# Output projection over head pairs, per-chunk scaling with a root taken as a power, and half-width masked products

## The chip, the cores and the metric

The kernel runs on one core of one Trainium2 chip. The metric is device time in microseconds (us) of one launch; the kernel before has a median of 3176.51 us in three runs. The engines go by the profile's names: PE is TensorE's matmul, PEld its weight load, DVE VectorE, ACT ScalarE, POOL GpSimd, SP the engine that issues most DMAs.

## What is computed

Two layers over 2048 tokens of width 1024, in float32. Layer 0 is a gated DeltaNet (GDN, 8 heads), layer 1 a gated linear attention (GLA, 4 heads); each head has key width 128 and value width 256. Cut to what the change touches:

```python
def gated_rmsnorm(o, w, gate):                 # per head, over its 256 values
    o = o * lax.rsqrt(jnp.mean(o * o, -1, keepdims=True) + RMS_EPS)
    return o * w * jax.nn.silu(gate)
def l2norm(t):                                 # q and k of GDN
    return t * lax.rsqrt(jnp.sum(t * t, -1, keepdims=True) + L2_EPS)
# mixer: p = x @ w_in (and a causal convolution of 4 taps for GDN); a recurrence over chunks gives o
y = gated_rmsnorm(o, norm_w, gate).reshape(B, T, heads * 256) @ w_out
x = layer_norm(DEEP_ALPHA * x + y, ln_g[i], ln_b[i])
```

## The kernel before

Work is cut into 48 units. A unit is one head of one layer on a group of 512 tokens, that is four chunks of 128 tokens (`NC`). There are 32 GDN units (4 groups, 8 heads) and 16 GLA units (4 groups, 4 heads). `PHASES` (L949) interleaves the layers: groups 0 and 1 of GDN, group 0 of GLA, and so on.

Four generators give the instructions (L936): `gemms` (input projection, convolution, gates), `preps` (what a head's recurrence needs: decays, inverses, masked products), `chains` (the recurrence itself) and `outs` (output projection, layer norm). `Plan.run` (L50 to L110) keeps a clock that adds up estimated matmul costs; a generator yields the time at which its next matmul can run, the first of the four that is due goes on, and `gemms` fills the rest. So the order in which each engine gets its instructions is fixed before the kernel runs, by the plan's costs (`COST`, L130) and by `O_GAP`, the least distance of two output groups. Every operation is issued inside the helper `Planned.call`, so the profile gives line L121 for all of them, and they are told apart by tile names.

Most products are float32 split in a high and a low part of a faster format (float32r): `mm3` (L234) issues three matmuls, high by high, high by low, low by high. Small products inside a head are plain float32, which the trace shows as two passes per matmul.

Tiles and names that the prediction's steps use:

- `wc`: a chunk of the input weights, both parts, 128 rows by up to 256 or 272 columns, in a ring of `W_BUFS` = 16. `Stream.load` (L261) brings the next chunk when one is free. The first time a weight is used it comes raw (`wraw`, ring of `RAW_BUFS` = 4), ACT makes the high part and POOL the low part, and the result is kept in DRAM (`wk`); later uses load that. `xh`, `xl` are the two parts of the transposed input, made by ACT and DVE from `woraw`.
- `psg` (three banks), `psc` (three), `psh` (one), `pso` (one): PSUM tiles of the projection, of a head's small products, of the recurrence and of the output projection.
- `gdn_prep` (L574): sums of squares of k and q go to `ss` (ACT), their inverse roots to `rr` (DVE, `rsqrt`); a 128 by 128 lower-triangular inverse is doubled from blocks of 16 to 128 with masked products `psc<-U,D` and `psc<-W,Tm` (L643 to L653 for the step from 16 to 32, at full width). `gla_prep` (L677) builds the intra-chunk matrix `At` over seven levels (L741 to L749); the levels with halves of 2, 4, 8 and 16 multiply full 128 by 128 tiles and merge what a mask picks with DVE's copy_predicated.
- `gdn_chain` (L790) and `gla_chain` (L815): per chunk, a read of the state (`psh<-S,kq`), `Rt` (DVE), `psh<-Rt`, `wt` (ACT copy), two products, and the new state `S` (DVE). `output` (L785) then takes the chunk's sum of squares (ACT Square into `junk`, `ssq`) and `og` = o times gate (DVE).
- `chains` (L828): after the fourth chunk, `z` = the RMS factor of all four chunks in one `rsqrt` on DVE (L834 to L845); `og` is transposed by PE and split to `oth`, `otl`. This waits in the plan until the unit before has finished its output projection.
- `outs` (L861): for each unit and each half `e` of the 1024 outputs, for each of four token tiles: two `mm3` (6 matmuls) into `pso`, then DVE computes y = pso * z + y. The weights `wo` (1024 KB with both parts, ring of `WO_BUFS` = 2) are loaded one ahead. After the last head of a group comes `layer_norm` (L918): bn_stats, bn_aggr, `rsqrt` of the variance on DVE, ACT scale and shift, DVE multiply and POOL add.
- `rsqrt` (L215): 11 DVE operations, two on the bits and three Newton steps of three, on tiles of 1, 4 or 8 columns:

```python
        v.tensor_scalar(yi, a.bitcast(I32), 1, None, ALU.logical_shift_right)
        v.tensor_scalar(yi, yi, -1.0, float(0x5F3759DF), ALU.mult, ALU.add)
        for _ in range(3):
            v.tensor_tensor(tmp, y, y, ALU.mult)
            v.scalar_tensor_tensor(tmp, tmp, -0.5, a, ALU.mult, ALU.mult)
            v.scalar_tensor_tensor(y, tmp, 1.5, y, ALU.add, ALU.mult)
```

Of the kernel before, what the change touches and what calls it, by code (L numbers as in the profile page):

```python
# [16 lines left out]
P = 128  # L17
# [7 lines left out]
DV = 256  # L25
QKV = 4096
ALPHA = 4.0 ** 0.25
BIG = 1.0e30
LEVELS = (1, 2, 4, 8, 16, 32, 64)
# [104 lines left out]
def trunk(ctx, tc, x, xT, w_in1, conv, a_log, dt_bias, nw1, w_out1, w_in2, gk_up, gk_b, nw2, w_out2,  # L134
# [46 lines left out]
    gkb = T("gkb", [P, H2])  # L181
    up = T("up", [80, 512], dt=F32R)
# [11 lines left out]
    def setup():  # L194
        sync.dma_start(nalog[:], a_log.unsqueeze(0).broadcast_to([P, H1]))
        sync.dma_start(dtb[:], dt_bias.unsqueeze(0).broadcast_to([P, H1]))
        sync.dma_start(cst[:].rearrange("p a b -> p (a b)"), consts)
        sync.dma_start(nws[0][:], nw1)
        s.activation(nalog[:], nalog[:], AF.Exp)
        v.tensor_scalar(nalog[:], nalog[:], -1.0, None, ALU.mult)  # L200
        v.tensor_reduce(id16[:], ident.rearrange("p (a b) -> p b a", b=16), mybir.AxisListType.X, ALU.add)
        for t in S1 + S2 + [halo]:
            v.memset(t[:], 0.0)

    def setup_gla():
        sync.dma_start(nws[1][:], nw2)
        sync.dma_start(gkb[:], gk_b)
        raw = T("th", [P, 512], 2)
        v.memset(raw[:], 0.0)
        for r0 in (0, 32, 64):  # L210
            sync.dma_start(raw[r0:r0 + 16, :], gk_up)
        s.copy(up[:], raw[:80, :])
        v.tensor_tensor(up[64:80, :], raw[64:80, :], up[64:80, :].bitcast(F32), ALU.subtract)

    def rsqrt(y, a, tmp):  # L215
        yi = y.bitcast(I32)
        v.tensor_scalar(yi, a.bitcast(I32), 1, None, ALU.logical_shift_right)
        v.tensor_scalar(yi, yi, -1.0, float(0x5F3759DF), ALU.mult, ALU.add)
        for _ in range(3):
            v.tensor_tensor(tmp, y, y, ALU.mult)  # L220
            v.scalar_tensor_tensor(tmp, tmp, -0.5, a, ALU.mult, ALU.mult)
            v.scalar_tensor_tensor(y, tmp, 1.5, y, ALU.add, ALU.mult)
# [26 lines left out]

    def prefetched(specs, load, ahead=1):  # L250
        ready = []
        specs = iter(specs)

        def take(ahead=ahead):
            while len(ready) <= ahead:
                spec = next(specs, None)
                ready.append(None if spec is None else load(spec))
            return ready.pop(0)
        return take
# [170 lines left out]
    take_wo = prefetched([c for u in units[:-1] for c in u.wo_specs()], load_wo)  # L430
# [142 lines left out]

    def gdn_prep(u):  # L574
# [16 lines left out]
        ss, r, tmp = small("ss", 2 * NC), small("rr", 2 * NC), small("rtmp", 2 * NC)  # L591
# [10 lines left out]
        v.tensor_scalar(ss[:], ss[:], 1e-6, None, ALU.add)  # L602
        rsqrt(r[:], ss[:], tmp[:])
        rk = r[:, 0:NC]
        rqs, brk, br2, s1 = (small(k, NC) for k in ("rqs", "brk", "br2", "s1"))
        v.tensor_scalar(rqs[:], r[:, NC:], float(P) ** -0.5, None, ALU.mult)
# [41 lines left out]
        d = PS("c", [P, NC, P])  # L648
# [26 lines left out]
        u.prep = dict(qd=qd, kd=kd, Bt=D2, Uf=Uf, s1=s1, rqs=rqs)  # L675

    def gla_prep(u):  # L677
# [63 lines left out]
        for lv, half in list(enumerate(LEVELS))[1:]:  # L741
            nxt = scaled(lv + 1) if lv + 1 < len(LEVELS) else None
            d = PS("c", [P, NC, P] if half < 32 else [P, NC, half])
            yield ready(d, E)
            if half < 32:
                for n in range(NC):
                    c = slice(n * P, (n + 1) * P)
                    mm(d[:, n], E[:, c], E[:, c])
                v.copy_predicated(At[:], bc(C(C_LV + lv), 1, NC).bitcast(I32), d)  # L749
            else:  # L750
                starts = range(0, P, 2 * half)
                for r0 in starts:
                    lo, hi = slice(r0, r0 + half), slice(r0 + half, r0 + 2 * half)
                    for n in range(NC):
                        e = E[:, n * P:(n + 1) * P]
                        mm(d[lo, n], e[:, lo], e[:, hi])
                for r0 in starts:
                    lo, hi = slice(r0, r0 + half), slice(r0 + half, r0 + 2 * half)
                    s.copy(At[lo, :, hi], d[lo])
            E = nxt  # L760
# [67 lines left out]
    def chains():  # L828
        for u in units:
            yield from after(("prep", u.at), ("vg", u.at))  # L830
            og, ssq = T("og", [P, NC, DV], 1), small("ssq", NC)
            yield from (gdn_chain if u.kind == 0 else gla_chain)(u, og, ssq)
            mark("rec", u.at)
            ms, z, tmp = small("ms", NC), small("z", NC), small("ztmp", NC)  # L834
            if u.kind == 1:
                v.tensor_scalar(ms[:], ssq[:], 1.0 / DV, 1e-6, ALU.mult, ALU.add)
                rsqrt(z[:], ms[:], tmp[:])
                v.tensor_scalar(z[:], z[:], 0.5 / ALPHA, None, ALU.mult)
            else:
                rqs = u.prep["rqs"][:]  # L840
                v.tensor_tensor(ms[:], rqs, rqs, ALU.mult)
                v.scalar_tensor_tensor(ms[:], ms[:], 1.0 / DV, ssq[:], ALU.mult, ALU.mult)
                v.tensor_scalar(ms[:], ms[:], 1e-6, None, ALU.add)
                rsqrt(z[:], ms[:], tmp[:])
                v.scalar_tensor_tensor(z[:], z[:], 0.5 / ALPHA, rqs, ALU.mult, ALU.mult)  # L845
            u.z = z
            end = u.at + 1 == len(units)
            if u.at and not end:
                yield from after(("out", u.at - 1))
            u.oT = []  # L850
            for j in range(2):
                d = PS("c", [P, NC, P])
                yield ready(d, og)
                transposes(d, lambda n: og[:, n, j * P:(j + 1) * P], NC)
                hi = T("D1" if end else "oth", [P, NC, P], 2, F32R)
                lo = T("D2" if end else "otl", [P, NC, P], 2, F32R)
                split(hi[:], lo[:], d)
                u.oT.append((hi, lo))
            mark("oT", u.at)

    def outs():  # L861
        for u in units:
            if u.first:
# [3 lines left out]
            end = u.at + 1 == len(units)  # L867
            wo = {}
            if u.at + 2 == len(units):
                wo = {e: take_wo(0) for e in range(2)}  # L870
                last = units[-1]
                yield from after(("vg", last.at))
                last_wo = {e: last_wo_parts(spec) for e, spec in enumerate(last.wo_specs())}
                gb = load_gb(last)
            if end:
                wo = last_wo
            yield from after(("oT", u.at))
            spaced = 0.0
            for e, n in [(e, n) for n in range(NC) for e in range(2)] if end else [(e, n) for e in range(2) for n in range(NC)]:
                final = u.last and e  # L880
                if e not in wo:
                    if final:
                        gb = load_gb(u)
                    wo[e] = take_wo(0 if final else WO_AHEAD)
                c = slice(e * 512, (e + 1) * 512)
                d = PS("g" if u.at + 2 >= len(units) else "o", [P, 512])
                for j in range(2):
                    hi, lo, _ = wo[e][j]
                    yield max(ready(d, u.oT[j][1], wo[e][j][2]), 0.0 if u.at + 2 >= len(units) or j else spaced)
                    if j == 0:  # L890
                        spaced = plan.clock + O_GAP
                    mm3(d, u.oT[j][0][:, n, :], u.oT[j][1][:, n, :], hi, lo, j == 0, j == 1)
# [4 lines left out]
            mark("out", u.at)  # L897
# [20 lines left out]
    def layer_norm(u, n, y, gb):  # L918
        st, mv = T("lnst", [P, 2, 6], 2), T("lnmv", [P, 2], 2)
        va, rs, tmp, mr = (small(k, 1, LN_BUFS) for k in ("lnva", "lnrs", "lntmp", "lnmr"))  # L920
# [3 lines left out]
        v.tensor_scalar(va[:], mv[:, 1:2], 1e-5 / ALPHA ** 2, None, ALU.add)  # L924
        rsqrt(rs[:], va[:], tmp[:])
# [14 lines left out]
W_BUFS, RAW_BUFS = 16, 4  # L940
WO_BUFS, WO_AHEAD, WO_RAW_BUFS = 2, 1, 4
# [48 lines left out]
```

## Time and profile before

| | us |
|---|---|
| three timed runs: lowest, median, highest | 3173.44, 3176.51, 3183.77 |
| the profiled execution, its own time | 3171.91 |
| span of its instructions | 3170.0 |
| PE busy (share of the span) | 3042.3 (96%) |
| PEld busy | 2578.7 (81%) |
| DVE busy | 2223.1 (70%) |
| ACT busy | 1181.8 (37%) |
| POOL busy | 388.8 (12%) |
| mean granted TensorE clock | 0.989 |

Busy time is the time in which at least one instruction of the engine was under way; matmuls overlap each other, so a busy PE may still be slower than it could be. Rows of a group read: line, engine, operation, output tile, input tiles, shape, count, busy time, mean ns of one, and the idle time of the engine just ahead of them with what ended it. Rows of the timeline read: start, duration, engine, operation, count, and in brackets the idle time before it and what ended that. Rows of waits give the total, the count and the longest.

### The profile page before, as it was taken

What the parts mean: (1) busy time and instruction counts of PE and PEld (TensorE: products, weight loads), DVE (VectorE), ACT (ScalarE), POOL (GpSimd) and SP (SyncE); (2) the same over time, 40 slices, a digit from 0 to 9 for tenths busy, and PEclk for the clock granted to TensorE, in tenths of its full rate; (3) what the DMA queues carried; (4) which work ended last, traced back from release to release, by engine and by line L of the source; (5) the groups of instructions that cost most, each with busy time, mean ns of one, the idle gap of its engine ahead of it and who ended that gap; (6) DMA issues with size and microseconds to landing.
All of it is one profiled execution on the core that took longest, in us unless ns stands there. A gap on an engine that the chain in (4) does not pass through costs nothing. (4 is left out here: it accounts for less than half of the span.)

```text
span 3170.0 us, 52680 instructions
## 1 busy us (share of the span) xinstructions
PE 3042.3 (96%) x18430; PEld 2578.7 (81%) x18430; DVE 2223.1 (70%) x6201; ACT 1181.8 (37%) x3091; POOL 388.8 (12%) x642
## 2 busy tenths in 40 slices
PE   9899999989999998998999999999999999999997
PEld 6678878778888877887888888888788888898895
DVE  6787777777677667578677757657877675755577
ACT  4444443332333445433333324523333233433331
POOL 4423220010000323102000000100200000100011
PEclk9999999999999999999999999999999999999998
DMA  7876565574444747665544553755645454465442
GB/s 236 258 238 213 183 194 180 162 223 150 141 131 146 226 125 250 215 201 184 163 143 141 152 167 101 232 179 164 192 148 155 153 159 131 152 193 173 147 161 105
DMA packets 442489, 551.93 MB, mean 174 GB/s; under 512 B 37568, under 2 KB 381888, under 8 KB 430192
## 3 DMA queue, kind: packets, MB, share of 16 engines
q1 hardware_dynamic: 412656, 505.57, 51.4%
q10 hardware_dynamic: 29568, 43.00, 4.0%
q8 instruction: 145, 2.38, 0.3%
q14 instruction: 120, 0.98, 0.1%
HBM read 421.24 MB, written 127.21 MB: 173 GB/s over the span
## 5 line engine op out<-in xcount | busy, mean ns | idle before, releaser
L121 PE MATMUL psg<-xh,wc 128*128 128x512 f32 x2560 | 886.9, 407 | 4.1 <-ACT wc L121 2.9
L121 PE MATMUL psg<-wc,xh 128*128 128x256 f32 (+1 forms) x4096 | 780.3, 289 | 24.3 <-DVE sg L121 14.3
L121 PEld LDWEIGHTS psg<-wc,xh 128*128 128x128 f32 x4096 | 654.4, 190 | 51.6 <-DVE sg L121 15.9
L121 PE MATMUL psg<-wc,xl 128*128 128x256 f32 (+1 forms) x2048 | 581.6, 284 | 0.0
L121 PEld LDWEIGHTS psg<-xh,wc 128*128 128x128 f32 x2560 | 480.2, 189 | 110.2 <-POOL wc L121 4.6
L121 PE MATMUL pso<-wo,oth 128*128 128x512 f32 x1472 | 506.8, 422 | 19.5 <-DVE y L121 17.0
L121 PE MATMUL psg<-xl,wc 128*128 128x512 f32 x1280 | 517.0, 404 | 0.4 <-DVE xl L121 0.3
L121 DVE SCALAR_TENSOR_TENSOR y<-pso,z,y 128x512 f32<-128x512 f32 x368 | 274.9, 747 | 188.8 <-PE pso L121 172.2
L121 PEld LDWEIGHTS psg<-wc,xl 128*128 128x128 f32 x2048 | 389.7, 190 | 1.3
L121 DVE SCALAR_TENSOR_TENSOR acc<-pb,taps,acc 128x512 f32<-128x512 f32 x384 | 301.6, 786 | 61.3 <-ACT acc L121 55.4
L121 PEld LDWEIGHTS pso<-wo,oth 128*128 128x128 f32 x1472 | 253.0, 189 | 67.7 <-DVE y L121 25.3
L121 PE MATMUL pso<-wo,otl 128*128 128x512 f32 x736 | 296.1, 402 | 0.5 <-DVE otl L121 0.5
L121 PEld LDWEIGHTS psg<-xl,wc 128*128 128x128 f32 x1280 | 241.8, 189 | 51.6 <-DVE xl L121 1.3
L121 POOL TENSOR_TENSOR wc<-wraw,wc 128x256 fp32r<-128x256 f32 (+1 forms) x288 | 231.4, 819 | 419.1 <-ACT wc L121 392.7
L121 ACT ACTIVATE th<-psg 128x256 f32<-128x256 f32 (+1 forms) x256 | 107.9, 434 | 349.5 <-PE psg L121 311.7
L121 ACT ACTIVATE junk<-psc 128x128 bf16<-128x128 f32 (+1 forms) x448 | 143.6, 321 | 219.6 <-PE psc L121 172.9
L121 DVE SCALAR_TENSOR_TENSOR sg<-th,psg 128x256 f32<-128x256 f32 x192 | 79.4, 415 | 145.6 <-ACT th L121 126.2
L121 POOL TENSOR_TENSOR y<-y,woraw 128x512 f32<-128x512 f32 x62 | 91.5, 1488 | 711.9 <-DVE y L121 324.4
L121 PEld LDWEIGHTS pso<-wo,otl 128*128 128x128 f32 x736 | 138.7, 188 | 37.1 <-DVE otl L121 6.1
L121 ACT ACTIVATE D<-D 128x512 f32<-128x512 f32 x160 | 100.0, 631 | 178.0 <-DVE D L121 140.2
L121 ACT COPY pb<-psg 128x512 f32<-128x512 f32 x128 | 74.9, 585 | 234.7 <-PE psg L121 227.7
L121 ACT CAST wc<-wraw 128x256 fp32r<-128x256 f32 (+1 forms) x288 | 112.1, 404 | 132.0 <-DMA wraw<-in_w_in 64.3
(182 smaller groups left out, 4454.5 us busy)
## 6 DMA issues: line engine op xcount, KB each, us to landing
wc<-wk SPq DMA_DIRECT2D x816, 256.0 KB
wk<-wc SPq DMA_DIRECT2D x272, 256.0 KB
wraw<-in_w_in SPq DMA_DIRECT2D x288, 128.0 KB
wo<-k_in_w_out SPq DMA_DIRECT2D x27, 1024.0 KB
wo<-_in_w_out SPq DMA_DIRECT2D x22, 1024.0 KB
wo<-ok_in_w_out SPq DMA_DIRECT2D x21, 1024.0 KB
Arep<-blk SPq DMA_DIRECT2D x32, 512.0 KB
wc<-wk SPq DMA_DIRECT2D x48, 272.0 KB
```

The source lines that it names most:

```text
L121: ins = op(*args, **kw)
```

## The change

1. **Pairs of units in the output projection.** `outs` goes over jobs: 23 pairs of units and two single units at the end. For each token tile and half `e`, four `mm3` (12 matmuls) of two heads accumulate in one bank, and one DVE add takes it to y. The scaling by `z` is gone from there. `WO_BUFS` is 3 and three `wo` tiles are asked for ahead; a job needs four, and the fourth is loaded only when its first half (`e` = 0) is done. `oth` and `otl` get four buffers each (`OT_BUFS`), and `chains` waits for the job of the unit two before.
2. **The root as a power, per chunk.** `rsqrt` is now an add of eps and a tensor_tensor with ALU.pow and a tile of -0.5 on POOL: 32 `rr`, 32 `lnrs` and 192 `z`. `z` is taken for each chunk right after its Square, from `ssq` and (for GDN) `qn`, a small DVE product of q's sum of squares, and ACT multiplies `og` by it. The constant factor moves to the `nw` tiles.
3. **Half width.** The step from 16 to 32 in `gdn_prep` and the levels 2 to 16 in `gla_prep` keep only those columns of the moving operand that the mask lets through: 64 in place of 128. The stationary operand stays 128 by 128. The DVE operations on these results have half the columns.
4. **Rings.** `W_BUFS` goes from 16 to 10, `RAW_BUFS` from 4 to 3. At the start, SP issues the fourth `wraw` load behind six more loads of `xT` and of small tables where it was the seventh DMA, and `cst` (the constants) is issued ahead of the seventh `wraw`.

The counts: PE 15923 instructions in the program before and after, DVE 6203 and 4566, ACT 2765 and 2957, POOL 647 and 1159, SP 1822 and 1822.

```diff
-    def rsqrt(y, a, tmp):
-        yi = y.bitcast(I32)
...
+    def rsqrt(y, a, eps):
+        if eps:
+            g.tensor_scalar(y, a, eps, None, ALU.add)
+        g.tensor_tensor(y, y if eps else a, mhalf[:, :y.shape[1]], ALU.pow)
...
+    jobs = [units[i:i + 2] for i in range(0, len(units) - 2, 2)] + [units[-2:-1], units[-1:]]
...
+    def later_half(a, sz):
+
+        if len(a.shape) == 2:
+            return a.rearrange("p (m h j) -> p m h j", h=2, j=sz)[:, :, 1, :]
+        return a.rearrange("p n (m h j) -> p n m h j", h=2, j=sz)[:, :, :, 1, :]
+
+    def halves(a, sz):
+        return a.rearrange("p n (m j) -> p n m j", j=sz)
...
-        v.tensor_scalar(ss[:], ss[:], 1e-6, None, ALU.add)
-        rsqrt(r[:], ss[:], tmp[:])
...
+        rsqrt(r[:], ss[:, :NC], 1e-6)
...
+        v.tensor_scalar(qn[:], ss[:, NC:], 1e-6, P * DV * 1e-6, ALU.add, ALU.mult)
...
         for n in range(NC):
-            mm(d[:, n], A[:, n], U[:, n])
-        v.tensor_tensor(W2[:], d, bc(C(C_LV + 4), 1, NC), ALU.mult)
-        d = PS("c", [P, NC, P])
+            mm(d[:, n], A[:, n], Uh[:, n])
+        v.tensor_tensor(Wh, d, bc(later_half(C(C_LV + 4), 16), 1, NC), ALU.mult)
+        d = halves(PS("c", [P, NC, P // 2]), 16)
         yield ready(d, W2)
         for n in range(NC):
-            mm(d[:, n], Tm[:, n], W2[:, n])
-        v.tensor_tensor(U[:], U[:], d, ALU.subtract)
+            mm(d[:, n], Tm[:, n], Wh[:, n])
+        v.tensor_tensor(Uh, Uh, d, ALU.subtract)
...
                 for n in range(NC):
-                    c = slice(n * P, (n + 1) * P)
-                    mm(d[:, n], E[:, c], E[:, c])
-                v.copy_predicated(At[:], bc(C(C_LV + lv), 1, NC).bitcast(I32), d)
+                    mm(d[:, n], E3[:, n], later_half(E3, half)[:, n])
+                v.copy_predicated(later_half(At[:], half), bc(later_half(C(C_LV + lv), half), 1, NC).bitcast(I32), d)
...
-        s.activation(jk[:], do, AF.Square, accum_out=ssq[:, n:n + 1])
+        c = slice(n, n + 1)
+        s.activation(jk[:], do, AF.Square, accum_out=ssq[:, c])
         v.tensor_tensor(og[:, n, :], do, u.sg[:, n, :], ALU.mult)
+        z = small("z", 1, 4)
+        if u.kind == 1:
+            g.tensor_scalar(z[:], ssq[:, c], DV * 1e-6, None, ALU.add)
+        else:
+            g.tensor_tensor(z[:], ssq[:, c], u.prep["qn"][:, c], ALU.add)
+        g.tensor_tensor(z[:], z[:], mhalf[:, :1], ALU.pow)
+        s.activation(og[:, n, :], og[:, n, :], AF.Copy, scale=z[:])
...
-            if u.at and not end:
-                yield from after(("out", u.at - 1))
+            if u.at >= 2 and not end:
+                yield from after(("out", units[u.at - 2].job))
...
+            parts = [(w, j) for w in job for j in range(2)]
             for e, n in [(e, n) for n in range(NC) for e in range(2)] if end else [(e, n) for e in range(2) for n in range(NC)]:
...
+                for k, (w, j) in enumerate(parts):
+                    hi, lo, wo = wos[w.at, e][j]
+                    yield max(ready(d, w.oT[j][1], wo), 0.0 if late or k else spaced)
...
+                    mm3(d, w.oT[j][0][:, n, :], w.oT[j][1][:, n, :], hi, lo, k == 0, k == len(parts) - 1)
                 y = ys[n]
-                v.scalar_tensor_tensor(y[:, c], d, u.z[:, n:n + 1], y[:, c], ALU.mult, ALU.add)
+                v.tensor_tensor(y[:, c], d, y[:, c], ALU.add)
+                if n == NC - 1 and not end:
+                    freed += len(job)
+                    if not final:
+                        fill()
...
-        v.tensor_scalar(va[:], mv[:, 1:2], 1e-5 / ALPHA ** 2, None, ALU.add)
-        rsqrt(rs[:], va[:], tmp[:])
+        rsqrt(rs[:], mv[:, 1:2], 1e-5 / ALPHA ** 2)
...
-W_BUFS, RAW_BUFS = 16, 4
-WO_BUFS, WO_AHEAD, WO_RAW_BUFS = 2, 1, 4
+W_BUFS, RAW_BUFS = 10, 3
+WO_BUFS, WO_RAW_BUFS, OT_BUFS = 3, 4, 4
```

How this moves the instructions is shown at two places. The first is ACT in the recurrence of a GDN unit, where `junk` is the Square, `wt` the copy that the next product waits for and `blk` a DMA that ACT issues. Before, it reads:

```order
L121 ACTIVATE junk_12049,ssq_11956<-psc_12044 128x256
L121 COPY wt_12064<-psh_12052 128x256
L121 ACTIVATE junk_12071,ssq_11956<-psc_12066 128x256
L121 COPY wt_12079<-psh_12074 128x256
L121 ACTIVATE junk_12110,ssq_11956<-psc_12081 128x256
L121 DMA blk_2717_12100<-X_12097 128x64
L121 COPY wt_12118<-psh_12113 128x256
L121 ACTIVATE junk_12125,ssq_11956<-psc_12120 128x256
```

And after, in the recurrence of a unit of the same kind:

```order
L122 ACTIVATE junk_9576,ssq_9496<-psc_9565 128x256
L122 ACTIVATE og_9495<-og_9495,z_9579 128x256
L122 COPY wt_9588<-psh_9583 128x256
L122 ACTIVATE junk_9613,ssq_9496<-psc_9590 128x256
L122 DMA blk_2198_9603<-X_9600 128x64
L122 ACTIVATE og_9495<-og_9495,z_9616 128x256
L122 COPY wt_9625<-psh_9620 128x256
L122 ACTIVATE junk_9632,ssq_9496<-psc_9627 128x256
L122 ACTIVATE og_9495<-og_9495,z_9635 128x256
L122 COPY wt_9644<-psh_9639 128x256
```

Between a Square and the next `wt` there is now the scaling of `og`, which waits for POOL's `z` of the same Square. In the whole program a scaling stands directly behind its Square 92 times of 192, and a `wt` directly behind a scaling 63 times of 128.

The second place is PE at one group of the output projection, where `oth` and `otl` are the two parts of the transposed `og`. Before, a group is two `mm3`:

```order
L121 MATMUL pso_6819<-wo_6445,oth_6432 128x512 x2
L121 MATMUL pso_6819<-wo_6445,otl_6433 128x512
L121 MATMUL pso_6819<-wo_6445,oth_6441 128x512
L121 MATMUL psc_6830<-W_1531_6365,Tm_6363 128x128 x4
L121 MATMUL pso_6819<-wo_6445,oth_6441 128x512
L121 MATMUL pso_6819<-wo_6445,otl_6442 128x512
```

And after, it is four, with two `wo` tiles (the last `mm3` of the group, on `oth_6951`, stands three rows after the last one shown here):

```order
L122 MATMUL pso_6982<-wo_5744,oth_6342 128x512 x2
L122 MATMUL pso_6982<-wo_5744,otl_6343 128x512
L122 MATMUL psg_6911<-xl_6204,wc_6633 128x512
L122 MATMUL psg_6911<-xh_6203,wc_6633 128x512
L122 MATMUL pso_6982<-wo_5744,oth_6351 128x512 x2
L122 MATMUL pso_6982<-wo_5744,otl_6352 128x512
L122 MATMUL psg_6911<-xh_6215,wc_6656 128x512
L122 MATMUL psg_6911<-xl_6216,wc_6656 128x512
L122 MATMUL psg_6911<-xh_6215,wc_6656 128x512
L122 MATMUL pso_6982<-wo_6135,oth_6942 128x512 x2
L122 MATMUL pso_6982<-wo_6135,otl_6943 128x512
```

The number of output matmuls is the same; the bank `pso` changes hands after 12 of them where it was 6.

More of the change, by code (lines that the diff above doesn't have):

```diff
@@ L866, in outs @@
                             else (lambda n: x2[u.gi][n][:]))
[L867 to L870, printed above, removed]
+            end, late = u.at + 1 == len(units), u.at + 2 >= len(units)
+            if late and not end:
                 last = units[-1]
                 yield from after(("vg", last.at))
[L873 removed]
+                for e, spec in enumerate(last.wo_specs()):
+                    wos[last.at, e] = last_wo_parts(spec)
@@ L919, in layer_norm @@
         st, mv = T("lnst", [P, 2, 6], 2), T("lnmv", [P, 2], 2)
-        va, rs, tmp, mr = (small(k, 1, LN_BUFS) for k in ("lnva", "lnrs", "lntmp", "lnmr"))
+        rs, mr = (small(k, 1, LN_BUFS) for k in ("lnrs", "lnmr"))
         for e in range(2):
```

92 lines of the change are left out of this document (39 added, 53 removed).

## The prediction

> **What bounds the kernel now.** I read the page first, for which engine is full.
>
> ```profile
> span 3170.0 us, 52680 instructions
> PE 3042.3 (96%) x18430; PEld 2578.7 (81%) x18430; DVE 2223.1 (70%) x6201; ACT 1181.8 (37%) x3091; POOL 388.8 (12%) x642
> ```
>
> PE is busy 96% of the span, so a change pays only where PE idles (3170.0 - 3042.3 = 128 us) or where PE's own work gets shorter. The second view, busy times by stretches (columns: length, PE, PEld, DVE, ACT, POOL, clock, DMA share, GB/s), tells where PE idles.
>
> ```profile
> 0.00:200.00 200.00, 175.17 (x946) 139.53 (x947) 137.35 (x316) 94.76 (x265) 85.95 (x129) 0.97 0.84 260
> 800.00:1000.00 200.00, 199.78 (x1167) 165.70 (x1166) 141.84 (x420) 65.19 (x200) 5.46 (x27) 1.00 0.48 144
> 3000.00:3170.00 170.00, 146.06 (x910) 128.03 (x909) 120.83 (x334) 45.63 (x97) 20.03 (x14) 0.94 0.42 140
> ```
>
> The first and the last stretch hold 24.8 + 23.9 = 49 us of it, a stretch in the middle 0.2 us, though DVE is busy 142 of 200 us there. The third view, what PE and its weight loads waited for (total, times, longest), names the releasers.
>
> ```profile
> PE pso L121 <- DVE y L121: 17.0, 18, 2.2
> PE psg L121 <- DVE sg L121: 15.8, 7, 7.2
> PE psc L121 <- DVE U L121: 14.5, 7, 5.7
> PE psh L121 <- DVE S L121: 14.0, 11, 3.2
> PE psg L121 <- ACT wc L121: 5.9, 5, 1.9
> PE psg L121 <- POOL wc L121: 3.4, 8, 1.0
> ```
> ```profile
> PEld psh L121 <- DVE S L121: 27.8, 47, 3.6
> PEld pso L121 <- DVE y L121: 25.3, 28, 2.5
> PEld psc L121 <- DVE U L121: 22.9, 29, 6.2
> ```
>
> DVE lies behind 61 us of PE's idle time in four rows, arriving weight chunks behind 9. A weight load stands earlier than the matmul behind it, while the last matmul's modelled end still counts as busy; what a wait really costs lies between the two rows, and I use their middle: y 21, S 21, U 19.
>
> **DVE's load.** These groups of DVE are touched.
>
> ```profile
> L121 DVE SCALAR_TENSOR_TENSOR y<-pso,z,y 128x512 f32<-128x512 f32 x368 | 274.9, 747 | 188.8 <-PE pso L121 172.2 <-issue 11.6
> ...
> L121 DVE SCALAR_TENSOR_TENSOR z<-ztmp,z 128x4 f32<-128x4 f32 x144 | 23.7, 164 | 2.9
> ...
> L121 DVE TENSOR_TENSOR W<-psc,cst 128x512 f32<-128x512 f32 x32 | 22.0, 689 | 13.2 <-PE psc L121 11.8
> ...
> L121 DVE TENSOR_SCALAR ms<-ssq 128x4 f32<-128x4 f32 x16 | 2.6, 163 | 0.0
> ```
> ```profile
> L121 DVE TENSOR_TENSOR og<-psc,sg 128x256 f32<-128x256 f32 x192 | 80.7, 421 | 9.2 <-ACT junk L121 6.5
> L121 DVE COPY_PREDICATED D<-cst,psc 128x512 f32<-128x512 int32 x64 | 47.0, 735 | 57.9 <-PE psc L121 57.9
> ```
>
> Evictions: 368 become 184, each of the kind of the 689 ns row, 127 us; 274.9 - 127 = -148. The root: 24 groups of small operations go, from `z<-ztmp,z` (23.7) to `ms<-ssq` (2.6), together 260 us; 32 `qn` at about 0.16 come back, 5. Half width: 64 operations of 689 ns go to the 421 ns of 256 columns, -17; 64 of 735 ns lose at most half, -23. Sum -148 - 255 - 17 - 23 = -443: DVE at about 1780 us, 56% of the span. None of this is the forecast, since it lies beside PE's work. What it buys is in the waits.
>
> **Waits on y (half of the hand-overs go).** Half as many at the same odds is -10 of 21; a DVE a fifth less loaded shortens the rest, -4. I take -14; bounds 0 (pairs wait as often) and -21.
>
> **Waits on sg, S and U (shorter queues on DVE).** `sg`, the gate's product, frees `psg`. Its longest wait is where a layer norm runs.
>
> ```profile
> 1494.90 1.23 DVE L121 SCALAR_TENSOR_TENSOR lnmr<-lnmv,lnrs 128x1 f32<-128x1 f32 x1
> ```
> ```profile
> 1493.13 2.98 POOL L121 TENSOR_TENSOR y<-y,woraw 128x512 f32<-128x512 f32 x2
> ```
> ```profile
> 1496.16 1.52 ACT L121 ACTIVATE y<-y,lnmr,lnrs 128x512 f32<-128x512 f32 x2 [3.09 <-DVE lnmr L121]
> ```
> ```profile
> 1502.97 0.80 PE L121 MATMUL psg<-wc,xh 128*128 128x256 f32 x2 [7.21 <-DVE sg L121]
> ```
>
> The root runs between other DVE work, `lnmr` comes late, ACT stands 3.09 us, and the gate behind it frees PE's bank 7.21 us late. With the root on POOL these steps leave DVE; but the next tile's pow stands behind the two POOL adds of the tile before, 2.98 us, so only part is won: -6 of 15.8. S and U are 40 us together, with DVE a fifth less loaded -9; bounds 0 and -20, half.
>
> **Half-width products: nothing on PE.** They are 512 matmuls, 1024 passes. Three bursts of the timeline tell what a pass costs.
>
> ```profile
> 46.93 0.53 PE L121 MATMUL psc<-lgz,cst 128*128 128x32 f32 x4
> ```
> ```profile
> 1043.94 1.05 PE L121 MATMUL psc<-U,D 128*128 128x128 f32 x8
> ```
> ```profile
> 1053.84 0.68 PE L121 MATMUL psc<-U,D 128*64 128x64 f32 x8
> ```
>
> With a stationary operand of 128 x 128, 32 moving columns took 0.53/4 = 0.133 us a pass and 128 columns 1.05/8 = 0.131; with 64 stationary columns it is 0.085. So a pass goes with the stationary operand, which stays at 128. I take 0; bounds 0 and 1024 x 0.046 = -47. The Trainium skill, "TensorE: Matmul & The Clock Gate", section "Back-to-back issue gap", gives an isolated gap of N / 2.4 + 2.5 ns, by which 64 columns fewer would save an estimated 27 ns a pass, 27 us in all; the same page's "LDWEIGHTS" section lets the load grow with the stationary columns, and this trace sides with that.
>
> **The root on POOL, and ACT held behind it (the added wait).** One turn of a GDN recurrence:
>
> ```profile
> 1002.17 0.38 ACT L121 ACTIVATE junk<-psc 128x256 bf16<-128x256 f32 x1 [1.28 <-PE psc L121]
> ...
> 1002.46 0.20 ACT L121 ACTIVATION_READ_ACCUMULATOR junk<-psc 128x1 f32 x1
> ...
> 1005.43 0.37 ACT L121 COPY wt<-psh 128x256 f32<-128x256 f32 x1 [2.78 <-DVE X L121]
> ...
> 1006.60 0.48 DVE L121 SCALAR_TENSOR_TENSOR S<-S,eg,psh 128x256 f32<-128x256 f32 x1 [0.52 <-PE psh L121]
> ...
> 1006.63 0.24 POOL L121 COPY X<-id 128x64 f32<-128x64 f32 x1 [38.41 <-DMA blk<-X]
> ```
> ```profile
> L121 ACT ACTIVATE y<-y,lnmr,lnrs 128x512 f32<-128x512 f32 x64 | 48.3, 806 | 79.0 <-DVE lnmr L121 49.3 <-DVE lnrs L121 21.6 <-POOL y L121 6.3
> ...
> L121 ACT ACTIVATE D<-U,brk 128x128 f32<-128x128 f32 x128 | 40.9, 390 | 1.0
> ```
> ```profile
> L121 POOL TENSOR_TENSOR y<-y,woraw 128x512 f32<-128x512 f32 x62 | 91.5, 1488 | 711.9 <-DVE y L121 324.4 <-DMA wc<-wk 246.5 <-DVE lnva L121 101.6
> ```
>
> The sum of squares is there at 1002.66, the next `wt` starts at 1005.43: 2.77 us. Into it must fit POOL's add, POOL's pow and ACT's scaling of 128x256 (between 390 and 806 ns, 0.5). That leaves 2.2 us for two POOL operations and some hand-overs. The trace has no pow; its nearest rows are a small copy at 0.24 us and a two-input add of 512 columns at 1.49. One column is nearest to the copy: 0.25 for the add, 0.4 for the pow, 1 us with hand-overs, and ACT is free 1.2 us early. The scalings add 192 x 0.5 = 96 us to an ACT that is 37% busy; where that, or a POOL queue with `wc` or layer-norm adds in it, falls on a `wt` or an `oth`, PE waits: +6 (bounds 0 and +76, the rival below). The 512 small POOL operations also run beside DVE: the S update at 1006.60 took its 0.48 us with a POOL copy beside it, the `lnmr` above 1.23 us beside large adds. I take 0. The Trainium skill, "GPSIMD Engine Reference", section "Key points", warns of POOL's sharing its SBUF interfaces with DVE instructions of two inputs; the large adds of this trace agree, the small copy does not show it.
>
> **Tail.** After the last matmul DVE finishes token tiles.
>
> ```profile
> 3152.97 1.22 DVE L121 SCALAR_TENSOR_TENSOR lnrs<-lntmp,lnrs 128x1 f32<-128x1 f32 x1
> ```
>
> Such small steps, drawn out like this one beside POOL's adds, leave DVE; POOL gets two operations a tile. I take -4, bounds 0 and -7.
>
> **Smaller rings.** With three raw buffers the fourth `wraw` waits in SP's queue.
>
> ```profile
> 3.71 0.43 SPq L121 DMA_DIRECT2D wraw<-in_w_in  x1
> ...
> 9.37 1.93 SPq L121 DMA_DIRECT2D wraw<-in_w_in  x4
> ```
> ```profile
> 13.81 0.50 PE L121 MATMUL psg<-xh,wc 128*128 128x512 f32 x1 [1.67 <-ACT wc L121]
> ```
>
> It goes from 3.71 to about where the next four stood, 9.37, and PE already waited for such chunks at 13.81: +5 (bounds 0 and +6). Later, arriving chunks cost 9.3 us in all. Ten buffers give six chunks less warning; half as much again is +4, the upper bound one longest wait of 1.0 us in each of 48 units, +48. The fourth `wo` tile is asked for half a job ahead, behind 24 output matmuls and what stands between them: +1.
>
> **Sum.** -14 - 6 - 9 - 4 + 0 + 6 + 5 + 4 + 1 = -17 us. The profiled execution took 3171.91 us, 4.6 under the median of 3176.51. The forecast is 3154.9 for such an execution and 3176.51 - 17 = 3159.5 as a median, -0.54%.
>
> **The rivals.**
>
> *Slow pow (slower).* Above about 1.6 us for the pow, ACT is still held when `wt` is due, and the recurrence, whose matmuls are in PE's fixed order, stands. A `wt` stands right behind a scaling 63 times. At 2.8 us each costs 1.2, 76 in all where I put 6: 3230. Against it: the 0.24 us copy. For it: no pow row.
>
> *Short rings (no change, or a little slower).* Chunk buffers fall by six of sixteen, and 0.84 of the DMA engines' time is taken in the first 200 us. Half of the bound of 48 is 24 where I put 4: 3180.
>
> *Narrow columns pay.* A pass at 0.085 us gives -47: 3113. The row of 32 columns speaks against it; it is one kind of row.
>
> *Queues empty faster.* DVE's waits at their bounds (-21 - 16 - 20 - 7) and the added terms at +16 give -48: 3129. The fall from 70% to 56% speaks for it; against it, such waits are mostly dependences.
>
> **How the numbers follow.** The forecast has 0.40, its own range is 3146 to 3172; short rings 0.18, queues 0.22, narrow columns 0.08, slow pow 0.12. About 0.3%, 9.5 us, is what a measurement of this kernel can tell from no change. Faster, below 3167: 0.28 of the forecast, queues and columns, 0.58. Same: 0.12 of the forecast and 0.09 of the rings, 0.21. Slower: 0.09 and the slow pow, 0.21. The range leaves out the slow pow and the ends of columns and rings: 3112 to 3190.
>
> **What would show it.** After: 184 `y<-pso` near 0.69 us; DVE near 1780 us; `PE pso <- DVE y` below 10 us; POOL's pow near 0.4 us and no wait of `psh` for `wt` above some 10 us; bursts of 128x64 at 0.13 us a pass, not 0.085; `wc` waits below 20 us; the first 200 us some 5 us idler. The forecast is wrong if PE's busy time falls by 40 us, or if waits on ACT's `og` or `wt`, or for chunks, pass 30 us.

## The result and the profile after

The changed kernel took 3253.62 us (median of 4 runs, 3246.03 to 3263.16), the kernel before 3174.98 (4 runs, 3170.21 to 3183.77). The ratio is 1.0238, 95% interval 1.0206 to 1.0271: slower by some 76 us, where I had forecast 17 us faster and a range that ended at 3190. Ratios leave disturbed runs out, so here and below a difference is (ratio - 1) x 3180, not the difference of two medians.

The page of the changed kernel, then its stretches (length, PE, PEld, DVE, ACT, POOL, clock, DMA share, GB/s):

```profile
span 3243.9 us, 51822 instructions
PE 3066.2 (95%) x18430; PEld 2612.1 (81%) x18430; DVE 1869.4 (58%) x4564; ACT 1273.0 (39%) x3283; POOL 612.8 (19%) x1154
```
```profile
0.00:200.00 200.00, 172.14 (x886) 141.83 (x887) 122.40 (x282) 94.34 (x262) 84.05 (x132) 0.90 0.73 230
200.00:400.00 200.00, 183.93 (x1045) 151.50 (x1045) 122.47 (x287) 89.50 (x243) 66.99 (x115) 0.96 0.59 186
400.00:600.00 200.00, 175.87 (x1004) 148.54 (x1004) 120.14 (x303) 84.17 (x235) 54.36 (x96) 0.94 0.57 183
800.00:1000.00 200.00, 198.94 (x1170) 168.24 (x1169) 118.22 (x315) 67.24 (x190) 19.33 (x58) 1.00 0.47 151
```

DVE is 354 us less busy, and PE idles 178 us where it idled 128. So 50 of the 74 us between the two spans are idle time of PE; the other 24 are PE's busy time, which grew from 3042.3 to 3066.2 with as many matmuls, at a mean clock of 0.977 for 0.989. The stretch from 800 to 1000 is as full as before. The loss begins early: by 200 us PE has done 886 matmuls where it had done 946, and from 200 to 600 it does 2049 where it did 2227, with a clock of 0.94 to 0.96. What PE waited for:

```profile
PE psh L122 <- DVE S L122: 28.6, 29, 2.9
PE psc L122 <- DVE og L122: 19.2, 4, 9.5
PE psg L122 <- DVE sg L122: 12.1, 5, 7.3
...
PE pso L122 <- DVE y L122: 7.8, 6, 3.6
PE psh L122 <- ACT wt L122: 7.8, 8, 1.5
```

The wait for evictions, `y`, fell from 17.0 to 7.8, but the waits inside a head's recurrence rose: S from 14.0 to 28.6, and `og` from 2.9 to 19.2 us, both times in four waits, now with one of 9.5. The pow, which the trace of before could not price, is here, with POOL's other new rows (mean ns behind the busy time):

```profile
L122 POOL TENSOR_TENSOR z<-z,mhalf 128x1 f32<-128x1 f32 x192 | 108.1, 563 | 15.4
...
L122 POOL TENSOR_TENSOR rr<-rr,mhalf 128x4 f32<-128x4 f32 x32 | 33.4, 1043 | 2.7
...
L122 POOL TENSOR_TENSOR z<-ssq,qn 128x1 f32<-128x1 f32 x128 | 27.9, 218 | 487.5 <-ACT junk L122 487.4
```

Add and pow together take 0.78 us, near my 0.65 and far from the 1.6 us for the pow alone from which the rival of the slow pow would decide.

The longest wait, read along the engines in the changed kernel: SP's queue, then ACT, then PE.

```profile
269.23 3.32 SPq L122 DMA_DIRECT2D woraw<-in_w_out  x4
275.34 1.08 SPq L122 DMA_DIRECT2D wraw<-in_w_in  x2
```
```profile
275.57 0.40 ACT L122 CAST wc<-wraw 128x256 fp32r<-128x256 f32 x1 [6.46 <-DMA wraw<-in_w_in]
...
281.60 0.41 ACT L122 CAST wc<-wraw 128x256 fp32r<-128x256 f32 x1 [5.62 <-DMA wraw<-in_w_in]
281.91 0.38 ACT L122 ACTIVATE junk<-psc 128x256 bf16<-128x256 f32 x1
```
```profile
282.89 0.69 PE L122 MATMUL psc<-cst,og 128*128 128x128 f32 x2 [9.54 <-DVE og L122]
283.46 0.79 PE L122 MATMUL psg<-xh,wc 128*128 128x512 f32 x1
```

ACT takes its instructions in order and stands 6.46 and 5.62 us at the casts of raw weight chunks that have not arrived; the Square behind them comes at 281.91, DVE's `og` behind it, and PE's next matmul, a transpose of `og`, waits for that. The same happens near 430 us: ACT stands 5.62 us at such a cast, and PE 8.35 us at `og`. Near 575 us it is a raw tile of `wo` that ACT waits for, 9.09 us, and PE stands 7.32 us at `sg`. So the loss had at least four suspects: the rings, ACT and POOL with the root per chunk, the pairs, and the half width.

### The profile page after: what moved, and what is told of

Its sections match the earlier page's. It is cut to its first block, busy times and chain, and to the rows that moved or that the text cites. A ratio compares the mean times of both kernels' runs of the same rounds, so it can differ in the third digit from the quotient of the medians.

```text
span 3243.9 us, 51822 instructions
## 1 busy us (share of the span) xinstructions
PE 3066.2 (95%) x18430; PEld 2612.1 (81%) x18430; DVE 1869.4 (58%) x4564; ACT 1273.0 (39%) x3283; POOL 612.8 (19%) x1154
## 5 line engine op out<-in xcount | busy, mean ns | idle before, releaser
L122 PE MATMUL psg<-xh,wc 128*128 128x512 f32 x2560 | 917.2, 412 | 7.0 <-ACT wc L122 4.3
L122 PE MATMUL psg<-wc,xh 128*128 128x256 f32 (+1 forms) x4096 | 803.0, 293 | 22.9 <-ACT xh L122 7.8
L122 PEld LDWEIGHTS psg<-wc,xh 128*128 128x128 f32 x4096 | 665.3, 191 | 63.7 <-ACT xh L122 8.4
L122 PEld LDWEIGHTS psg<-xh,wc 128*128 128x128 f32 x2560 | 486.8, 191 | 114.6 <-ACT wc L122 5.1
L122 PE MATMUL pso<-wo,oth 128*128 128x512 f32 x1472 | 494.7, 416 | 12.6 <-DVE y L122 7.5
L122 DVE TENSOR_TENSOR y<-pso,y 128x512 f32<-128x512 f32 x184 | 126.0, 685 | 127.0 <-PE pso L122 126.8
L122 ACT CAST wc<-wraw 128x256 fp32r<-128x256 f32 (+1 forms) x288 | 114.1, 404 | 194.7 <-DMA wraw<-in_w_in 126.2
L122 ACT ACTIVATE og<-og,z 128x256 f32<-128x256 f32 x192 | 97.6, 508 | 162.3 <-POOL z L122 95.7
```

Source lines behind the costliest of these rows:

```text
L122: ins = op(*args, **kw)
```

## The experiments

All times below are against the kernel before on the same chip. First, each part by itself. The rings alone (10 and 3), then each ring alone (16 and 3, 10 and 4):

```diff
-W_BUFS, RAW_BUFS = 16, 4
+W_BUFS, RAW_BUFS = 10, 3
```

> The kernel before with W_BUFS, RAW_BUFS = 10, 3 and nothing else of the change. Ring theory (the smaller rings make raw weight chunks late, and ACT, which takes its instructions in order, stands at the cast of a late chunk with the recurrence's work behind it): +45 to +80 us over the kernel before, most of it gained in the first 600 us, ACT's waits for wraw near 126 us and longest 7 us as in the changed kernel (64 and 3.7 before). ACT theory (the per-chunk scaling on ACT, which waits for POOL's root, delays wt and the transposes) and pair theory (the order of the paired output projection): within 10 us of the kernel before.

Measured: 1.0056 (1.0037 to 1.0075), +18 us. Neither branch holds: the rings cost something, but a quarter of the loss.

> The kernel before with rings 16 and 3. If the raw ring makes the rings' loss at the start: +10 to +16 us, nearly all in the first 100 us. If the chunk ring does: within 4 us of the kernel before.

> The kernel before with rings 10 and 4. If the chunk ring makes the later part of the rings' loss: +4 to +10 us, in the reloads (PE's weight loads waiting for DMA), none in the first 100 us. If the raw ring makes all of it: within 4 us.

Measured: 1.0013 (0.9996 to 1.0029) for the raw ring, +4 us, and 1.0042 (1.0030 to 1.0054) for the chunk ring, +13 us. They add up to the +18; the second is a little above its 4 to 10. The raw ring, on which my prediction put its 5 us at the start, is the lesser; with ten chunk buffers PE's weight loads wait for reloads, a row that the kernel before does not have:

```profile
PEld psg L121 <- DMA wc<-wk: 15.7, 10, 5.5
```

The root as a power with the scaling per chunk (part 2 of the change on the kernel before: `rsqrt`, `qn`, `output`, and an eviction that only adds):

> The kernel before with the root as a power on POOL and the scaling of og per chunk on ACT, rings 16 and 4, single heads, full width. ACT theory: +40 to +75 us, with the waits of the recurrence (S, wt, og) grown as in the changed kernel. Ring theory and pair theory: no slower than the kernel before; DVE loses some 255 us of work, which gives -5 to -25 us.

Measured: 1.0072 (1.0056 to 1.0087), +23 us. Neither branch holds: it is not the whole loss, and it is no gain either.

The half width alone (`later_half`, `halves` and the two places that use them):

> The kernel before with the half-width products alone. By the prediction (a pass goes with the stationary operand): PE's busy time unchanged within 5 us, time 0 to -10 us. If the moving width decided: -47 us. None of the ring, ACT and pair theories expects it to be slower.

Measured: 0.9960 (0.9947 to 0.9973), -13 us, a little more than the 10 expected, and the one part that pays by itself. PE's busy time did not fall:

```profile
PE 3049.1 (96%) x18430; PEld 2588.7 (82%) x18430; DVE 2203.1 (69%) x6201; ACT 1182.5 (37%) x3091; POOL 387.2 (12%) x642
```

Parts 2 and 3 together, without pairs and with the rings of before:

> The changed kernel without pairs and with rings 16 and 4: root on POOL, scaling per chunk, half width, single heads. Ring theory and pair theory: -10 to -40 us against the kernel before. ACT theory: +40 to +75 us.

Measured: 1.0059 (1.0044 to 1.0073), +19 us, between its two branches and 9 more than the two parts add up to (+23 and -13). Now the same with one root for the four chunks of a unit (`z` of 128x4), applied in the eviction as before:

```diff
-        g.tensor_tensor(z[:], z[:], mhalf[:, :1], ALU.pow)
-        s.activation(og[:, n, :], og[:, n, :], AF.Copy, scale=z[:])
...
+            g.tensor_tensor(z[:], z[:], mhalf[:], ALU.pow)
...
-                v.tensor_tensor(y[:, c], d, y[:, c], ALU.add)
+                v.scalar_tensor_tensor(y[:, c], d, u.z[:, n:n + 1], y[:, c], ALU.mult, ALU.add)
```

> The kernel before with half width and the root as a power on POOL, but z once per unit (128x4) and applied in the eviction as before: no scaling on ACT. Rings 16 and 4, single heads. Scaling theory (the loss of the root per chunk comes from ACT, where the scaling waits for POOL's z ahead of wt): -15 to -35 us against the kernel before, below the half-width kernel's -13. If the root on POOL itself costs (its queue, its port): +5 to +20 us, like the kernel with root per chunk and half width.

Measured: 0.9957 (0.9943 to 0.9972), -14 us, the same as half width alone. Two things follow. Putting the roots on POOL costs nothing and brings nothing in sum:

```profile
PE 3041.6 (96%) x18430; PEld 2594.5 (82%) x18430; DVE 2018.8 (64%) x4748; ACT 1182.0 (37%) x3091; POOL 520.8 (16%) x866
```

DVE is 184 us less busy than with half width alone, and the time is the same. And the scaling per chunk, the difference to the +19, costs 33 us. Why it does was asked three times. First with a constant in place of `z`, so that ACT does not wait for POOL; the RMS factor is left out of this kernel's output:

```diff
-        s.activation(og[:, n, :], og[:, n, :], AF.Copy, scale=z[:])
+        s.activation(og[:, n, :], og[:, n, :], AF.Copy, scale=0.0625)
```

> The kernel with root per chunk and half width (single heads, rings 16 and 4), but ACT scales og by a constant, so it doesn't wait for POOL's z; z is computed and not used. It leaves the RMS factor out of the output. Hold theory (ACT stands between Square and wt until POOL's z is there): 15 to 30 us faster than with z, -15 to 0 against the kernel before. Occupancy theory (192 more ACT operations of 0.5 us in the way): within 8 us of the kernel with z, +12 to +27.

Measured: 1.0059 (1.0041 to 1.0077), +19 us, as with `z`. The hold theory falls, and with it the term that my prediction had put on this. Then with the scaling on POOL:

```diff
-        s.activation(og[:, n, :], og[:, n, :], AF.Copy, scale=z[:])
+        g.tensor_scalar(og[:, n, :], og[:, n, :], z[:], None, ALU.mult)
```

> The same kernel with the scaling of og on POOL behind the pow, none on ACT. If the loss is ACT's (hold or occupancy): -20 to 0 us against the kernel before, like the kernel with one root per unit. If it is that the transposes get og later: as slow as with the scaling on ACT or slower, +15 to +40.

Measured: 1.0079 (1.0059 to 1.0099), +25 us. POOL takes 995 ns for a scaling where ACT took 507, so `og` is later still, and PE's weight loads wait 39.6 us for it where they waited 24.3. ACT's time is not the cause either: these loads wait 17.4 us for `wt` here, 20.8 with the scaling on ACT and 19.7 with one root per unit. What is left is that `og` is ready later, on the chip or in the plan that orders PE's work. The last of the three issues the same instructions past the plan:

```diff
...
-            g.tensor_tensor(z[:], ssq[:, c], u.prep["qn"][:, c], ALU.add)
-        g.tensor_tensor(z[:], z[:], mhalf[:, :1], ALU.pow)
-        s.activation(og[:, n, :], og[:, n, :], AF.Copy, scale=z[:])
+            nc.gpsimd.tensor_tensor(z[:], ssq[:, c], u.prep["qn"][:, c], ALU.add)
+        nc.gpsimd.tensor_tensor(z[:], z[:], mhalf[:, :1], ALU.pow)
+        nc.scalar.activation(og[:, n, :], og[:, n, :], AF.Copy, scale=z[:])
```

> The kernel with root per chunk and half width (single heads, rings 16 and 4), with z and the scaling of og issued past the plan: the plan takes og as ready when DVE has made it, so PE's order is close to that of the kernel with one root per unit, while the instructions are the same. Order theory (the plan, told of a later og, moves the transposes and the output projection to places where PE waits more): -5 to -20 us against the kernel before, like one root per unit. Latency theory (og is later on the chip, whatever the order): +19 or more.

Measured: 1.0024 (1.0014 to 1.0035), +8 us, between the two. Some 11 of the 33 us lie in the plan's order. For the other 22, the waits of PE's weight loads for `og`, with one root per unit and with the scaling past the plan:

```profile
PEld psc L122 <- DVE og L122: 10.1, 9, 4.8
```
```profile
PEld psc L122 <- ACT og L807: 27.0, 31, 8.1
```

The transposes stand 17 us longer for a scaled `og` by this row, and 9 by PE's own (17.0 for 7.9); the truth lies between, and the rest of the 22 is open. POOL's 288 additional small operations do not slow DVE's updates of S, which take 476 ns with `z` per chunk and with one root per unit. The split into 11 and 22 is rough, since the two orders differ in other places too.

Now the pairs. Without them, all else as in the change:

> The changed kernel without the pairs: root per chunk, half width, rings 10 and 3, single heads. Pair theory (the paired projection brings the rest of the loss): the parts add, 18 + 19 = +37 us over the kernel before. If the rest comes from the rings and the root together (raw chunks' casts and POOL's roots in the same queues): +65 to +80 us.

Measured: 1.0126 (1.0111 to 1.0141), +40 us: the rings' 18 and the 19 of the other two parts add. The changed kernel once more, on another chip:

> The changed kernel itself, so that the others can be set against it on one chip: +65 to +85 us over the kernel before.

Measured: 1.0235 (1.0213 to 1.0256), +75 us. So the pairs, on which I had put -14, bring +35. Two kernels go at the long stalls, one with a fourth raw buffer (and a chunk buffer less, for the memory), one that asks for the `wo` tiles one at a time:

```diff
-W_BUFS, RAW_BUFS = 10, 3
+W_BUFS, RAW_BUFS = 9, 4
```

> The changed kernel with rings 9 and 4 in place of 10 and 3 (what the memory holds). If the third raw buffer makes the three stalls of 7 to 10 us between 270 and 580 us: 25 to 35 us faster than the changed kernel, +40 to +50 over the kernel before. If the two wo tiles that a pair fetches and stores at once make them: within 10 us of the changed kernel.

Measured: 1.0199 (1.0184 to 1.0213), +63 us, 12 less than the change and less than expected. ACT's wait for raw chunks falls from 126.2 to 77.8 us, but the tenth chunk buffer is missed: the weight loads wait 33.3 us for reloads, where they waited 7.4 in the change:

```profile
ACT wc L122 <- DMA wraw<-in_w_in: 77.8, 53, 8.4
```
```profile
PEld psg L122 <- DMA wc<-wk: 33.3, 33, 3.5
```

```diff
-        def fill():
+        def fill(most=1):
...
-                    if not final:
-                        fill()
+                if n % 2 and not final and not end:
+                    fill()
...
```

> The changed kernel with its wo tiles asked for one at a time, behind every second token tile, where it asks for two at once. If two tiles at once (their raw loads, scalings and stores) make the three stalls: 20 to 35 us faster than the changed kernel. If the rings or ACT's order make them: within 10 us of it.

Measured: 1.0184 (1.0164 to 1.0203), +59 us, 16 less than the change: short of the 20 to 35, and 19 us above the kernel without pairs. Two combinations with it, the `wo` tiles one at a time in both, did not help:

> The changed kernel with wo tiles one at a time and the scaling on POOL. If the parts' losses add (scaling 32, two tiles at once 18): +20 to +30 us over the kernel before. If pairs cost by themselves, whatever the scaling and the loads: +45 us or more.

> The changed kernel with wo tiles one at a time and with z and the scaling issued past the plan. Order theory: 20 to 35 us faster than with the wo tiles one at a time alone, +25 to +40 over the kernel before. Latency theory: +58 or more.

Measured: 1.0300 (1.0278 to 1.0323), +95 us, with the scaling on POOL, and 1.0207 (1.0194 to 1.0220), +66 us, with the scaling past the plan, which had helped the single heads. So the pairs cost by themselves, whatever the scaling and the loads, and the theory of the plan's order, which asked for +25 to +40, fails in the paired kernel; the +66 lies in the range of the latency theory, +58 or more. That left open why pairs cost, and I looked at where the output matmuls stand. Busy time of the tile `pso` by 20 us, PE's share with its count first: before, then in the changed kernel.

```profile
280.00:300.00 20.00, 5.45 (x17) 3.05 (x15) 1.49 (x2) 0.00 (x0) 0.94 0.75 226
300.00:320.00 20.00, 5.48 (x19) 3.09 (x18) 2.28 (x4) 0.00 (x0) 0.97 0.76 248
320.00:340.00 20.00, 2.40 (x7) 1.43 (x8) 1.47 (x2) 0.00 (x0) 1.00 0.36 118
```
```profile
280.00:300.00 20.00, 0.00 (x0) 0.00 (x0) 0.00 (x0) 0.00 (x0) 0.82 0.51 163
300.00:320.00 20.00, 0.00 (x0) 0.00 (x0) 0.00 (x0) 0.00 (x0) 0.95 0.78 240
320.00:340.00 20.00, 0.00 (x0) 0.00 (x0) 0.00 (x0) 0.00 (x0) 0.88 0.50 154
```

Before, each 20 us hold some output matmuls. After, a stretch of 60 us holds none: a job's matmuls were all put close together ahead of it. The longest wait, 273 to 283 us, runs into this stretch, and the one near 430 us lies in the next, 420 to 460, which holds none either. The reason stands in the constant that the change left alone. `O_GAP`, the plan's least distance of two output groups, is 7050; a group became twice as long and a job of two heads has as many groups as one head had, so it is through in the time of one.

```diff
-O_GAP = 7050
+O_GAP = 14100
```

> The changed kernel with its wo tiles one at a time and the plan's distance of two output groups doubled to 14100, so that the twice as long groups stand as far apart, by their work, as before. Density theory (12-matmul groups at the old distance crowd the recurrence's and the projection's work): 10 to 20 us faster than with one tile at a time alone, +38 to +48 over the kernel before. If density is not it: within 8 us of +58.

Measured, with the `wo` tiles one at a time: 1.0105 (1.0087 to 1.0124), +33 us, a larger gain than the +38 to +48 expected. And the constant alone:

> The changed kernel with the plan's distance of two output groups doubled to 14100 and nothing else (two wo tiles at once, as in the change). If density and the double fetch are two causes that add: 75 - 25 = +50 over the kernel before. If density is the one cause and the fetch only matters when groups are crowded: +30 to +38, like with one tile at a time.

Measured: 1.0106 (1.0086 to 1.0126), +34 us. The doubled distance takes 41 of the 75 us away by itself, and fetching one tile at a time adds nothing to it. The output matmuls are spread again, and PE's stretch from 200 to 600 us, 2049 matmuls in the change, holds 2250. The first 200 us are not won back: they hold 870, and 896 with the smaller rings alone, where the kernel before has 946.

```profile
280.00:300.00 20.00, 5.17 (x18) 3.39 (x18) 1.31 (x2) 0.00 (x0) 1.00 0.55 171
300.00:320.00 20.00, 3.63 (x12) 1.96 (x12) 0.71 (x2) 0.00 (x0) 1.00 0.78 260
320.00:340.00 20.00, 1.83 (x6) 0.98 (x6) 0.00 (x0) 0.00 (x0) 1.00 0.63 195
```
```profile
200.00:600.00 400.00, 385.92 (x2250) 320.27 (x2250) 268.12 (x624) 185.29 (x509) 127.76 (x222) 1.00 0.62 195
```

With that, the account of the change, step by step from kernel to kernel, is: half width -13, roots on POOL 0, scaling per chunk +33, smaller rings +21 (the kernel without pairs against the one with the rings of before), the pairs at a fitting distance -6 (+34 against +40, whose intervals overlap), the crowding +41; together +76. Such a chain closes whatever the parts do to each other; tried alone, the rings cost 18, and root and scaling 23 on top of the kernel before. Whether the kernel before would gain from another distance was not tried. The two kernels that beat both are the single-head ones with half width, with the root on DVE (0.9960) or on POOL per unit (0.9957).

## Why the prediction was wrong

The forecast has no term for where the longer output groups stand in time, and that is the largest part of the loss. Its signs did not show it: 184 evictions of 685 ns, `y` below 10 us and bursts at 0.125 us a pass came as named, and neither sign of being wrong did. PE's busy time rose by 24 us instead of falling by 40, and PE's waits on ACT's `og` (8.3), on `wt` (7.8) and for chunks (7.4 + 4.7 + 4.9) stayed below 30 us each.

*The y term* (-14). The step held where it looked: PE's waits on `y` fell from 17.0 to 7.8 us and the evictions from 368 of 747 ns to 184 of 685. What failed is that the pairs' cost was looked for only at the hand-over of the bank and at the fourth `wo` tile (+1). The output matmuls depend on nothing that the recurrence is doing just then; spread through it, they are what PE runs while streamed weights, Squares and `og` are on their way. Crowded by an `O_GAP` that no longer fitted, they were used up in part of each job's time, and late chunks, Squares and roots stood uncovered after it. The raw chunk at 275.57 us is the trigger of the longest wait, and the missing cover is why it cost PE 9.54 us: with the doubled distance ACT still waits 103.1 us for raw chunks, once for 10.7, while PE's waits for `og` on DVE fall from 19.2 to 8.1 and PE idles 157 us in place of 178. The kernel before with three raw buffers fits this: ACT's wait for raw chunks rises from 64.3 to 120.0 us there, and the time by 4.

The waits inside the recurrence are another matter. With the doubled distance the first row stays and the second falls:

```profile
PE psh L122 <- DVE S L122: 29.1, 24, 3.1
...
PE psc L122 <- DVE og L122: 8.1, 5, 4.7
```

So the rise of S from 14.0 us is not the crowding's, and PE's wait for `Rt`, next in that chain, even rises from 2.7 to 19.1. The wait on S is 16.5 with one root per unit and 22.9 with the scaling per chunk, in both without pairs.

*The S, U and sg terms* (-15). They took a lighter DVE to mean shorter waits, and shorter waits to mean time. In the changed kernel U fell from 14.5 to 3.3 us and `sg` from 15.8 to 12.1, but S rose by 14.6, about as much as both fell. The lighter DVE by itself shows in half width alone against one root per unit, 184 us of DVE apart. PE's waits on `y` and `sg` in the first, then three rows of the second:

```profile
PE pso L121 <- DVE y L121: 20.8, 20, 2.4
PE psg L121 <- DVE sg L121: 18.5, 8, 6.3
```
```profile
PE psh L122 <- DVE S L122: 16.5, 17, 2.9
...
PE pso L122 <- DVE y L122: 9.4, 11, 2.0
...
PE psg L122 <- DVE sg L122: 4.6, 6, 2.5
```

Both fell, and the time is the same: PE idles 126 us where it idled 122, since other waits grew, the one on `D` from 0.4 to 14.6 us, on S from 11.5 to 16.5, on `og` from 2.6 to 7.9. The plan's order of PE's work differs in the two as well, and no run separates why they grew. For S the groups, before and with one root per unit, tell more by the idle time at their end:

```profile
L121 DVE SCALAR_TENSOR_TENSOR S<-S,eg,psh 128x256 f32<-128x256 f32 x128 | 61.0, 477 | 33.0 <-PE psh L121 30.0 <-PE psc L121 1.5
```
```profile
L122 DVE SCALAR_TENSOR_TENSOR S<-S,eg,psh 128x256 f32<-128x256 f32 x128 | 60.9, 476 | 59.4 <-PE psh L122 55.8 <-PE psc L122 2.6
```

DVE stood ahead of S and waited for `psh`; a lighter DVE only waits longer there. The rival "queues empty faster" fails with these terms: queues did empty faster, and it brought no time.

*The half-width term* (0 on PE). The mechanism was right. The burst in the changed kernel:

```profile
313.88 1.00 PE L122 MATMUL psc<-U,D 128*128 128x64 f32 x8
```

That is 0.125 us a pass, where 128 columns took 0.131 and a stationary operand of 64 columns 0.085. The part still pays 13 us. By these bursts 1024 x 0.006 = 6 of them can be the passes; the shorter DVE operations between two products (423 ns for 689) are the likely rest, which is argued and not shown.

*The term for ACT held behind POOL's root* (+6, the rival up to +76). The sizes of the operations were near (pow 0.56 us for 0.4, scaling 508 ns for 0.5 us), and the hold is not what costs: the constant scale is as slow. In its place, `og` comes later to the transposes, and the plan, which knows it, moves PE's order: 33 us together, some 11 by the order and between 9 and 17 by the later `og`, the rest open. The slow-pow rival named 3230 us, the nearest to the result, by a mechanism that did not happen; its nearness is luck.

*The rings* (+9, the rival up to +24). The measured +18 to +21 lie near the short-rings rival's price. The chunk ring does most of it, and part of it falls at the start after all: with both rings smaller PE has done 896 matmuls by 200 us where it had done 946, with either one smaller 926 and 928.

*The tail* (-4) held. From the end of the last matmul to the end of the span it is 22.1 us before and 19.2 in the changed kernel, 22.1 with half width alone and 19.4 with one root per unit.

## What to carry to other kernels

When a unit of filler work changes size, the constants that space it belong to the change: look at where the independent matmuls stand in time before and after, not only at how many there are. Busy time taken from an engine off the critical path is worth nothing by itself: its queues can empty faster, as for `y` and `sg` here, and waits elsewhere take their place. And price a pipeline step by what waits for its result, here the transposes, as well as by what stands behind it on its engine.

## What the runs showed of the hardware

A long wait of PE costs twice. The clock in the changed kernel around the 9.54 us wait:

```profile
270.00:276.00 6.00, 3.21 (x18) 2.20 (x16) 2.44 (x7) 0.40 (x1) 0.05 (x1) 1.00 1.02 359
276.00:283.00 7.00, 0.11 (x1) 0.11 (x2) 0.44 (x2) 1.40 (x6) 1.59 (x3) 0.56 0.78 295
283.00:290.00 7.00, 6.86 (x24) 5.06 (x25) 4.45 (x14) 3.60 (x9) 1.97 (x4) 0.71 0.47 150
```

The granted clock fell to 0.56 and was still 0.71 in the 7 us in which PE had work again; by 7 x (1 - 0.71) an estimated 2 us of matmul time were lost on top of the wait. The mean clock of the run fell from 0.989 to 0.977. The Trainium skill, "TensorE: Matmul & The Clock Gate", section "HAM oscillation — how this bites in real kernels", says that a gap above about 3.4 us throttles the array again; this gap of 9.54 us agrees, and no run here shows the threshold itself.

The removed DVE work was smaller than its rows add up to. Small operations of DVE overlap:

```profile
1488.37 0.14 DVE L121 SCALAR_TENSOR_TENSOR lntmp<-lntmp,lnva 128x1 f32<-128x1 f32 x1
1488.44 0.14 DVE L121 TENSOR_SCALAR lnrs<-lnva 128x1 int32<-128x1 int32 x1
```

They last 0.14 us and start 0.07 us apart, so a sum of their durations overstates the busy time: 255 us in my working, where 184 us went with the roots. Half width took 20 us from DVE where I had 40, so DVE stands at 1869 us and not at 1780.
